# Feed-forward block of layer 1: the first two blocks of hidden channels are opened together, each with its two products that need half of the channels

## The chip, the cores and the metric

The kernel runs on one core of one Trainium2 chip, as a single program that computes the whole step. The metric is the device time of an execution in microseconds, as the median of the runs. The profile is one execution of the same program, taken by the hardware profiler on that core.

## The reference

One inference step of a decoder of two layers, for 512 prompt tokens and 8 sequences of 8 new tokens. Layer 0 mixes by a short convolution and attention to a memory, layer 1 by block-sparse attention with compressed, selected and sliding-window branches. Behind each mixer come an output projection, the residual, and a feed-forward block (FFN) of gated kind. What matters here is the part from the output projection to the end of a layer's FFN:

```python
D_MODEL = 1024
D_FF = 2816

def rmsnorm(x, g):
    y = x * lax.rsqrt(jnp.mean(x * x, axis=-1, keepdims=True) + RMS_EPS)
    return y * g

def swiglu(h, w_gu, w_dn):
    gate, up = jnp.split(h @ w_gu, 2, axis=-1)
    return (jax.nn.silu(gate) * up) @ w_dn

# in each layer, x is the residual of shape (tokens, 1024)
x = x + y @ w_o[l]
x = x + swiglu(rmsnorm(x, g_ffn[l]), w_gu[l], w_dn[l])
```

This is a cut in plain words of the functions, with the casts left out; all is float32.

## The kernel before, in words

**Layout.** The residual is held transposed: eight tiles `c.x[0]` to `c.x[7]` of 128 channels by 576 columns, a column for each of the 512 + 64 tokens. The columns are worked in two halves of 288. Every float32 product is made of three TensorE products: each operand is split into a high and a low part (`c.split`: ScalarE makes the high part at L185, VectorE the low part at L186), and high x high, high x low and low x high are summed in PSUM.

**The FFN's blocks.** `_ffn` goes through 22 blocks of the hidden channels (groups `FFG` of 4, 4, 4, 4, 3, 3). A block is 128 gate and 128 up channels, whose weights (1024 x 256) come in one load to `wq` (two buffers). `_seven` computes a block by seven products instead of eight: weights and columns are cut into two by two quarters, `a11` to `a22` for the weights (gate or up, lower or upper channels) and `b11` to `b22` for the columns (channels by half of the tokens), and each product takes a sum or difference of quarters on either side. A product is twelve matmuls of 128 x 128 by 128 x 288 (four slices of channels, three parts each) into one PSUM bank; the banks are taken by turns from the tags `d` and `s`, two banks each. The sums of weights are made by GpSimd in place (L723 to L728, `s3` having one buffer), each sum is split once more (L185, L186), and a product's result goes through `part` tiles (six of 288 columns): ScalarE copies it at L711, VectorE adds it at L715, GpSimd sums two at L735.

**The columns' side.** `_factors` makes seven factors `f[0]` to `f[6]` when they are first asked for: `b11`, `b21`, `t2`, `t3`, `t4`, `t1`, `b22`, with `t1 = b12 - b11` (tiles `ob` and `oa` hold their parts). The lower channels, `b11` and `b12`, come from the residual's tiles 0, 1, 4 and 5 only, so `f[0]` and `f[5]` need these four; all other factors need 2, 3, 6 and 7 as well. The output projection of layer 1, `_project_o`, goes through its columns in the order

```python
    for cc in (0, 2, 1, 3):
```

so that the tiles 0, 1, 4 and 5 are final before the last quarter of the projection runs.

**The root.** The norm's factor isn't multiplied into the columns but into the results: `evac` multiplies by the tile `rs` (L776 and L778, on GpSimd, with the sigmoid-weighted gate between them on ScalarE, L777), adds and multiplies on VectorE (L775, L780, L781), and splits the product for the second matrix. `rs` is made from the sums of squares by ten small matmuls (L230), a chain of small VectorE steps (L239 to L245, tile `rm`), five transposes on TensorE (L190) and copies on ScalarE and VectorE (L271, L274). In layer 0 it is made ahead of the FFN but for the copies; in layer 1 it is made when the first `evac` asks for it, in the middle of the first products.

**What sets the order.** Each engine runs its instructions in order. Which order that is, a scheduler of the tile framework decides when the program is built: it takes the code in the order in which it is written, and its own estimate of when operands and buffers come free, and lays down one list for each engine. More buffers, or code written in another order, can therefore move instructions that the diff doesn't name. The load of block j + 2's weights waits on SP's queue until the splits of block j have read `wq`. From the second group on, the second matrix's products of the group before (`dn`) are woven between a block's.

Of the kernel before, what the change touches and what calls it, by code (L numbers as in the profile page):

```python
# [22 lines left out]
KD = D // P  # L23
# [14 lines left out]
        "tmp": NT, "sq": NT, "rs": NT, "rm": 24, "sm": 32, "ss": 16, "sl": 16, "oa": NT, "ob": NT, "tf": 2 * NT,  # L38
        "wq": 2048, "wd": 1024, "bh": NT, "bl": NT, "wh": 512, "wl": 512, "s3": 512, "part": HALF, "ah": NT, "al": NT, "lh": 384, "ll": 384}
BUFS = {"x": 2, "v0": 4, "v1": 8, "v2": 8, "v3": 8, "raw": 2, "hi": 3, "lo": 3, "sp": 7, "pt": 4, "tmp": 3, "sq": 5,  # L40
        "rm": 2, "sm": 6, "ss": 6, "sl": 4, "oa": 14, "ob": 14, "tf": 7, "wq": 2, "wd": 2, "bh": 2, "bl": 2, "wh": 6, "wl": 6, "part": 6,
        "ah": 6, "al": 6, "lh": 8, "ll": 8}


# [636 lines left out]
    return pairs  # L681


def _seven(c, w, f, evac):


    nc = c.nc

    def quarter(a):
        a = a.rearrange("p (q h j) c -> p h q j c", h=2, j=2)  # L690
        return a[:, 0], a[:, 1]

    def unit(src):
        h, l = (c.t(t, dt=F32R).rearrange("p (q j c) -> p q j c", q=2, j=2) for t in ("wh", "wl"))
        c.split(h, l, src)
        return h, l

    def product(src, b):
        b = [b(q) for q in range(2)]
        u = unit(src)  # L700
        ps = c.psum(next(c.seven))[:, :HALF]
        for k in range(4):
            for x, y in ((0, 0), (0, 1), (1, 0)):
                nc.tensor.matmul(ps, u[x][:, k // 2, k % 2], b[k // 2][y][:, k % 2], start=(k == 0 and x + y == 0),  # L704
                                 stop=(k == 3 and x == 1))
        return ps

    def part(ps):
        t = c.t("part")
        nc.scalar.activation(t, ps, AF.Copy)  # L710
        return t  # L711

    def total(ps, t):
        out = c.t("part")
        nc.vector.tensor_tensor(out, ps, t, op=ALU.add)  # L715
        return out

    (a11, a12), (a21, a22) = quarter(w[:, :, :P]), quarter(w[:, :, P:])
    t1 = part(product(a11, f[0]))
    yield  # L720
    evac(0, 0, product(a12, f[1]), t1, c.t("part"))
    s3 = c.t("s3").rearrange("p (q j c) -> p q j c", q=2, j=2)
    nc.gpsimd.tensor_tensor(s3, a11, a21, op=ALU.subtract)  # L723
    nc.gpsimd.tensor_tensor(a21, a21, a22, op=ALU.add)
    nc.gpsimd.tensor_tensor(a11, a21, a11, op=ALU.subtract)  # L725
    yield
    u2 = total(product(a11, f[2]), t1)
    nc.gpsimd.tensor_tensor(a12, a12, a11, op=ALU.subtract)  # L728
    yield
    u3 = total(product(s3, f[3]), u2)  # L730
    yield
    evac(1, 0, product(a22, f[4]), u3, c.t("part"))
    yield
    t5 = part(product(a21, f[5]))
    nc.gpsimd.tensor_tensor(u2, u2, t5, op=ALU.add)  # L735
    yield
    evac(0, 1, product(a12, f[6]), u2, u2)
    evac(1, 1, u3, t5, t5)
    yield
# [16 lines left out]
def _ffn(c, layer, f, rs, op=()):  # L756
# [3 lines left out]
    w, wd = io["w_gu"][layer], io["w_dn"][layer]  # L760
    act = {}
    banks = itertools.cycle("tote")

    def gu(j):
        a = c.t("wq")
        nc.sync.dma_start(a, w[j])
        gt = c.t("tmp")
        tags = ("ah", "al") if j % 8 < 6 else ("bh", "bl")
        act[j] = h, l = [c.t(t, dt=F32R) for t in tags]

        def evac(m, n, x, y, out):
            o = slice(n * HALF, (n + 1) * HALF)
            g, r = gt[:, o], rs()[:, o]
            if m == 0:
                nc.vector.tensor_tensor(g, x, y, op=ALU.add)  # L775
                nc.gpsimd.tensor_tensor(g, g, r, op=ALU.mult)  # L776
# [2 lines left out]
            else:  # L779
                nc.vector.tensor_tensor(out, x, y, op=ALU.add)  # L780
                nc.vector.tensor_tensor(g, out, g, op=ALU.mult)  # L781
                c.split(h[:, o], l[:, o], g)
        return _seven(c, a.rearrange("p (k c) -> p k c", k=KD), f, evac)

    def acts(f0, f1):
        return [act[j][0] for j in range(f0, f1)], [act[j][1] for j in range(f0, f1)]
# [41 lines left out]

    left, pace, due = iter(()), 0.0, 0.0
    for i, (f0, f1) in enumerate(FFG):  # L830
        for j in range(f0, f1):
            for n, _ in enumerate(gu(j)):
                if i and j == f0 and n == 2:
                    left, pace, due = dn(*FFG[i - 1]), 16 / (7.0 * (f1 - f0) - 2), 0.0
                    next(left)
# [916 lines left out]
```

## Time and profile before

| what | us |
|---|---|
| median of 3 runs | 1660.23 (1657.28 to 1665.26) |
| the profiled execution, own time | 1662.34 |
| its span in the trace | 1660.6 |
| TensorE (PE) busy | 1590.8, 12036 matmuls |
| VectorE (DVE) busy | 1219.3 |
| ScalarE (ACT) busy | 783.5 |
| GpSimd (POOL) busy | 618.0 |

The mean granted clock of TensorE over the span is 0.982 of its full speed. Times in the trace count from the span's start. The first products of layer 0's FFN stand at about 372 us, those of layer 1's at about 1237 us. A busy time holds all the time that an instruction was in its engine, also what it spent there standing still.

### The profile page before, as it was taken

The numbers are of one execution on the slowest core, as the hardware profiler recorded it, in microseconds if no ns is written. First come the engines' busy times: TensorE is split into PE (matmuls) and PEld (weight loads), VectorE is DVE, ScalarE is ACT, GpSimd is POOL, SyncE is SP. The second block draws the span as 40 slices with busy tenths as digits, with TensorE's granted clock in tenths as the row PEclk, the third lists the DMA queues.
The fourth block names the chain that finished last, engine by engine and source line by source line (L and its number), as shares of the span: only waits on it lengthen the run. The fifth ranks groups of instructions, "written<-read, shape, count | busy, mean of one in ns | idle before, by whom it ended". The sixth has DMA issues, their size and how long they took to land.

```text
span 1660.6 us, 32051 instructions
## 1 busy us (share of the span) xinstructions
PE 1590.8 (96%) x12036; PEld 1477.6 (89%) x12036; DVE 1219.3 (73%) x2520; ACT 783.5 (47%) x1728; POOL 618.0 (37%) x652
## 2 busy tenths in 40 slices
PE   7999999998999999999999999999998999999996
PEld 7879999888999999998996866666898999999996
DVE  7665464749988888886456476787668988889886
ACT  5542242644344444443255376677645434444444
POOL 5011022318666565540000021121256756565541
PEclk8999999999999999999999999999998999999998
DMA  7412383242222322223145465665012132232221
GB/s 250 171 48 77 129 264 102 71 162 77 83 96 89 103 89 79 96 84 137 51 166 166 164 186 162 199 187 176 27 55 99 64 115 77 92 100 90 74 80 57
DMA packets 65348, 190.72 MB, mean 115 GB/s; under 512 B 9350, under 2 KB 16810, under 8 KB 54570
## 3 DMA queue, kind: packets, MB, share of 16 engines
q1 hardware_dynamic: 63848, 187.48, 34.0%
q8 instruction: 95, 1.56, 0.4%
q10 hardware_dynamic: 1346, 1.21, 0.3%
q14 instruction: 59, 0.48, 0.1%
HBM read 169.86 MB, written 18.80 MB: 114 GB/s over the span
## 4 chain that ended last, share of the span: by engine, by line
PE 84%; DVE 7%; DMA 3%; issue 2%; ACT 2%; SPq 0%; DVEq 0%; ACTq 0%
PE psd L704 14%; PE pss L704 14%; PE psd L197 6%; PE psd L198 6%; PE psd L199 6%; PE pss L461 4%; PE pso L1222 3%; PE pst L190 3%; PE pst L197 3%; PE pst L199 3%; PE pst L198 3%; PE psd L1165 2%; PE pse L1351 2%; PE pse L198 2%; PE pse L199 2%
## 5 line engine op out<-in xcount | busy, mean ns | idle before, releaser
L186 DVE TENSOR_TENSOR wl<-wq,wh 128x512 fp32r<-128x512 f32 x280 | 268.5, 966 | 19.2 <-ACT wh L185 13.3
L197 PE MATMUL psd<-v,hi 128*128 128x288 f32 (+2 forms) x720 | 216.4, 303 | 14.0 <-ACT hi L185 7.8
L198 PE MATMUL psd<-v,hi 128*128 128x288 f32 (+2 forms) x720 | 215.9, 300 | 2.6 <-DVE v L295 2.5
L199 PE MATMUL psd<-v,lo 128*128 128x288 f32 (+2 forms) x720 | 215.3, 300 | 2.1 <-DVE lo L186 2.1
L185 ACT ACTIVATE wh<-wq 128x512 fp32r<-128x512 f32 x280 | 169.6, 623 | 88.3 <-PE psd L704 25.9
L197 PEld LDWEIGHTS psd<-v,hi 128*128 128x128 f32 (+1 forms) x720 | 136.7, 191 | 18.9 <-ACT hi L185 7.9
L198 PEld LDWEIGHTS psd<-v,hi 128*128 128x128 f32 (+1 forms) x720 | 137.3, 191 | 5.7 <-DVE v L295 3.3
L199 PEld LDWEIGHTS psd<-v,lo 128*128 128x128 f32 (+1 forms) x720 | 136.9, 191 | 5.1 <-DVE lo L186 2.7
L704 PE MATMUL psd<-ob,wh 128*128 128x288 f32 x616 | 127.7, 298 | 5.1 <-DVE tmp L775 3.3
L704 PE MATMUL psd<-oa,wh 128*128 128x288 f32 x616 | 127.6, 298 | 2.7 <-DVE part L715 2.4
L704 PE MATMUL pss<-oa,wh 128*128 128x288 f32 x616 | 128.1, 299 | 2.0 <-DVE part L715 2.0
L704 PE MATMUL pss<-ob,wh 128*128 128x288 f32 x616 | 127.0, 297 | 2.8 <-DVE part L715 0.9
L781 DVE TENSOR_TENSOR tmp<-part,tmp 128x288 f32<-128x288 f32 x88 | 89.4, 1015 | 53.6 <-POOL tmp L778 49.4
L776 POOL TENSOR_TENSOR tmp<-tmp,rs 128x288 f32<-128x288 f32 x88 | 95.5, 1085 | 84.6 <-DVE tmp L775 84.5
L185 ACT ACTIVATE hi<-raw 128x1024 fp32r<-128x1024 f32 (+3 forms) x60 | 59.9, 1003 | 119.3 <-PE psd L198 104.3
L704 PEld LDWEIGHTS psd<-ob,wh 128*128 128x128 f32 x616 | 100.1, 190 | 6.5 <-DVE tmp L775 3.7
L704 PEld LDWEIGHTS psd<-oa,wh 128*128 128x128 f32 x616 | 100.4, 191 | 3.9 <-issue 1.9
L704 PEld LDWEIGHTS pss<-ob,wh 128*128 128x128 f32 x616 | 99.8, 190 | 4.3 <-DVE ob L186 1.2
L704 PEld LDWEIGHTS pss<-oa,wh 128*128 128x128 f32 x616 | 101.3, 192 | 2.4 <-DVE part L715 2.4
L186 DVE TENSOR_TENSOR lo<-raw,hi 128x1024 fp32r<-128x1024 f32 (+3 forms) x60 | 75.3, 1261 | 26.0 <-ACT hi L185 25.8
L777 ACT ACTIVATE part<-tmp 128x288 f32<-128x288 f32 x88 | 39.2, 445 | 114.0 <-POOL tmp L776 113.8
L725 POOL TENSOR_TENSOR wq<-wq 128x512 f32<-128x512 f32 x44 | 59.2, 1346 | 89.5 <-DVE wl L186 89.5
(474 smaller groups left out, 4950.8 us busy)
## 6 DMA issues: line engine op xcount, KB each, us to landing
wq<-in_w_gu SPq DMA_DIRECT2D x44, 1024.0 KB
g<-in_cmp_pages SPq DMA_DIRECT2D x64, 256.0 KB
wd<-in_w_dn SPq DMA_DIRECT2D x32, 512.0 KB
raw<-in_w_in_a SPq DMA_DIRECT2D x9, 1024.0 KB
v<-in_cache_mem_kv SPq DMA_DIRECT2D x32, 256.0 KB
x<-in_slc_pages SPq DMA_DIRECT2D x32, 256.0 KB
raw<-in_slc_pages SPq DMA_DIRECT2D x32, 256.0 KB
wd<-in_w_dn SPq DMA_DIRECT2D x16, 384.0 KB
```

Of the source, the lines that this page charges most:

```text
L185: self.nc.scalar.activation(hi, src, AF.Copy)
L186: (eng or self.nc.vector).tensor_tensor(lo, src, hi.bitcast(F32), op=ALU.subtract)
L190: self.nc.tensor.transpose(out, in_, self.ident[:k, :k])
L197: nc.tensor.matmul(out, wh, xh, start=(k == 0), stop=False)
L198: nc.tensor.matmul(out, wh, xl, start=False, stop=False)
L199: nc.tensor.matmul(out, wl, xh, start=False, stop=(k == n - 1))
L461: nc.tensor.matmul(ps[:, :n], w[kv][i][:, lt, 2 * kp + k], x[j][:, k, lt:lt + n], start=(kp + k + lt + i + j == 0), stop=(kp == 3 and k + ...
L704: nc.tensor.matmul(ps, u[x][:, k // 2, k % 2], b[k // 2][y][:, k % 2], start=(k == 0 and x + y == 0), stop=(k == 3 and x == 1))
L725: nc.gpsimd.tensor_tensor(a11, a21, a11, op=ALU.subtract)
L776: nc.gpsimd.tensor_tensor(g, g, r, op=ALU.mult)
L781: nc.vector.tensor_tensor(g, out, g, op=ALU.mult)
L1222: nc.tensor.matmul(po()[64 * s:64 * s + 64, :P], v, w, start=(i + j == 0), stop=(i == 1 and j == len(todo) - 1))
```

## The change

For the first two blocks of layer 1, `_ffn` starts both at once, and by turns: first product of block 0, of block 1, then a second one of block 0 and of block 1. With `early`, `_seven` takes as its second product `t5 = a21' x f[5]` (`a21'` being the sum of L724) and `a12 x f[1]` behind it, with the first `evac`; without it `t5` stays where it was, the sixth. All 22 blocks of both layers go through the same code, but `early` is set for these two alone. `part` has eight buffers instead of six, `s3` two instead of one, in both layers, and the gate's tile `gt` is taken when the first `evac` needs it, after `rs`. No instruction is added or taken away, and none changes in size.

```diff
--- before.py
+++ after.py
@@ -38,7 +38,7 @@
-        "rm": 2, "sm": 6, "ss": 6, "sl": 4, "oa": 14, "ob": 14, "tf": 7, "wq": 2, "wd": 2, "bh": 2, "bl": 2, "wh": 6, "wl": 6, "part": 6,
+        "rm": 2, "sm": 6, "ss": 6, "sl": 4, "oa": 14, "ob": 14, "tf": 7, "wq": 2, "wd": 2, "bh": 2, "bl": 2, "wh": 6, "wl": 6, "part": 8, "s3": 2,
@@ -681,7 +681,8 @@
-def _seven(c, w, f, evac):
+def _seven(c, w, f, evac, early=False):
@@ -718,10 +719,15 @@
     (a11, a12), (a21, a22) = quarter(w[:, :, :P]), quarter(w[:, :, P:])
     t1 = part(product(a11, f[0]))
     yield
-    evac(0, 0, product(a12, f[1]), t1, c.t("part"))
+    if not early:
+        evac(0, 0, product(a12, f[1]), t1, c.t("part"))
     s3 = c.t("s3").rearrange("p (q j c) -> p q j c", q=2, j=2)
     nc.gpsimd.tensor_tensor(s3, a11, a21, op=ALU.subtract)
     nc.gpsimd.tensor_tensor(a21, a21, a22, op=ALU.add)
+    if early:
+        t5 = part(product(a21, f[5]))
+        yield
+        evac(0, 0, product(a12, f[1]), t1, c.t("part"))
     nc.gpsimd.tensor_tensor(a11, a21, a11, op=ALU.subtract)
     yield
     u2 = total(product(a11, f[2]), t1)
@@ -730,8 +736,10 @@
     u3 = total(product(s3, f[3]), u2)
     yield
     evac(1, 0, product(a22, f[4]), u3, c.t("part"))
-    yield
-    t5 = part(product(a21, f[5]))
+    if not early:
+        yield
+    if not early:
+        t5 = part(product(a21, f[5]))
     nc.gpsimd.tensor_tensor(u2, u2, t5, op=ALU.add)
     yield
     evac(0, 1, product(a12, f[6]), u2, u2)
@@ -761,16 +769,17 @@
     act = {}
     banks = itertools.cycle("tote")
 
-    def gu(j):
+    def gu(j, early=False):
         a = c.t("wq")
         nc.sync.dma_start(a, w[j])
-        gt = c.t("tmp")
+        gt = _Lazy(lambda: c.t("tmp"))
         tags = ("ah", "al") if j % 8 < 6 else ("bh", "bl")
         act[j] = h, l = [c.t(t, dt=F32R) for t in tags]
 
         def evac(m, n, x, y, out):
             o = slice(n * HALF, (n + 1) * HALF)
-            g, r = gt[:, o], rs()[:, o]
+            r = rs()[:, o]
+            g = gt()[:, o]
             if m == 0:
...
@@ -780,7 +789,7 @@
...
-        return _seven(c, a.rearrange("p (k c) -> p k c", k=KD), f, evac)
+        return _seven(c, a.rearrange("p (k c) -> p k c", k=KD), f, evac, early)
@@ -828,8 +837,14 @@
 
     left, pace, due = iter(()), 0.0, 0.0
     for i, (f0, f1) in enumerate(FFG):
+        ahead = []
+        if layer == 1 and i == 0:
+            ahead = [gu(j, True) for j in range(2)]
+            for _ in range(2):
+                for g in ahead:
+                    next(g)
         for j in range(f0, f1):
-            for n, _ in enumerate(gu(j)):
+            for n, _ in enumerate(ahead.pop(0) if ahead else gu(j)):
                 if i and j == f0 and n == 2:
                     left, pace, due = dn(*FFG[i - 1]), 16 / (7.0 * (f1 - f0) - 2), 0.0
                     next(left)
```

The lists of the engines show what this moves at three places. A name carries its tile's number, which the two kernels count differently. Lines up to L684 have the same number in both; behind it the changed kernel's are 1 to 9 higher (L704 is L705, L723 is L725, L776 is L785).

On GpSimd, at the opening of layer 0's FFN (`wq_475` holds block 0's weights there, `wq_507` block 1's), the list was:

```order
L723 TENSOR_TENSOR s3_487_4737<-wq_475_4691 128x512
L724 TENSOR_TENSOR wq_475_4691<-wq_475_4691 128x2x2x128
L725 TENSOR_TENSOR wq_475_4691<-wq_475_4691 128x2x2x128
L728 TENSOR_TENSOR wq_475_4691<-wq_475_4691 128x2x2x128
L723 TENSOR_TENSOR s3_519_4893<-wq_507_4847 128x512
L776 TENSOR_TENSOR tmp_476_4693<-tmp_476_4693,rs_472_4637 128x288
L724 TENSOR_TENSOR wq_507_4847<-wq_507_4847 128x2x2x128
L778 TENSOR_TENSOR tmp_476_4693<-part_486_4732,rs_472_4637 128x288
L725 TENSOR_TENSOR wq_507_4847<-wq_507_4847 128x2x2x128
```

And it is now:

```order
L725 TENSOR_TENSOR s3_487_4737<-wq_475_4691 128x512
L725 TENSOR_TENSOR s3_519_4893<-wq_507_4847 128x512
L726 TENSOR_TENSOR wq_475_4691<-wq_475_4691 128x2x2x128
L726 TENSOR_TENSOR wq_507_4847<-wq_507_4847 128x2x2x128
L731 TENSOR_TENSOR wq_475_4691<-wq_475_4691 128x2x2x128
L734 TENSOR_TENSOR wq_475_4691<-wq_475_4691 128x2x2x128
L785 TENSOR_TENSOR tmp_486_4732<-tmp_486_4732,rs_472_4637 128x288
L731 TENSOR_TENSOR wq_507_4847<-wq_507_4847 128x2x2x128
L787 TENSOR_TENSOR tmp_486_4732<-part_485_4731,rs_472_4637 128x288
```

The two sums of block 1 (L723 and L724, now L725 and L726) stand ahead of the third sum of block 0 and of its first multiplication by `rs_472`, where the first of them stood behind four of block 0 and the second behind that multiplication.

On TensorE, at the opening of layer 1's FFN, the first row of each product is given, from the first product behind the projection to the transposes (`oa` and `ob` are the factors' parts). It was:

```order
L704 MATMUL psd_2460_15970<-ob_2453_15955,wh_2458_15966 128x288
...
L704 MATMUL pss_2470_16003<-ob_2463_15988,wh_2468_15999 128x288
...
L704 MATMUL psd_2486_16079<-ob_2480_16061,wh_2484_16075 128x288
...
L230 MATMUL pss_2472_16017<-ones_2_68,tmp_2395_15499 128x1
...
L704 MATMUL pss_2495_16110<-ob_2489_16097,wh_2493_16106 128x288
L704 MATMUL psd_2504_16140<-oa_2498_16127,wh_2502_16136 128x288
...
L704 MATMUL pss_2512_16170<-oa_2506_16158,wh_2510_16166 128x288
...
L190 MATMUL pst_2475_16036<-ident_1_63,rm_2473_16028 128x128 x4
...
L704 MATMUL psd_2520_16198<-oa_2514_16186,wh_2518_16194 128x288
```

And it is now:

```order
L705 MATMUL psd_2462_15973<-ob_2455_15958,wh_2460_15969 128x288
...
L705 MATMUL pss_2466_15992<-ob_2455_15958,wh_2464_15988 128x288
...
L705 MATMUL psd_2476_16029<-oa_2470_16014,wh_2474_16025 128x288
...
L705 MATMUL pss_2481_16051<-oa_2470_16014,wh_2479_16047 128x288
...
L705 MATMUL psd_2491_16084<-ob_2484_16069,wh_2489_16080 128x288
...
L230 MATMUL pss_2493_16098<-ones_2_68,tmp_2395_15499 128x1
...
L705 MATMUL psd_2515_16182<-ob_2509_16169,wh_2513_16178 128x288
L705 MATMUL pss_2506_16151<-ob_2500_16136,wh_2504_16147 128x288
...
L705 MATMUL psd_2532_16243<-oa_2526_16231,wh_2530_16239 128x288
L705 MATMUL pss_2524_16212<-oa_2518_16199,wh_2522_16208 128x288
...
L190 MATMUL pst_2496_16117<-ident_1_63,rm_2494_16109 128x128 x4
...
L705 MATMUL pss_2535_16278<-ob_2484_16069,wh_2533_16274 128x288
```

There were 72 matmuls of `_seven` ahead of the first transpose (row 7792 of TensorE's list) and there are 103 (row 7823); the ten small matmuls of L230 stood inside the third product, from behind 27 matmuls on, and stand behind the fifth product's twelfth, behind 60.

On VectorE, at the same opening, around the first step of the root's chain (L239); `wq_2448` is block 0 of layer 1. Rows 1909 to 1918 were:

```order
L186 TENSOR_TENSOR wl_2519_16195<-wq_2448_15947,wh_2518_16194 128x512
L775 TENSOR_TENSOR tmp_2449_15949<-pss_2470_16003,part_2461_15983 128x288
L649 TENSOR_TENSOR tf_2497_16125<-v0_2465_15992,tf_2478_16053 128x576
L186 TENSOR_TENSOR wl_2526_16235<-wq_2521_16229,wh_2525_16234 128x512
L186 TENSOR_TENSOR ob_2483_16072<-tf_2478_16053,ob_2482_16071 128x576
L186 TENSOR_TENSOR oa_2492_16103<-tf_2488_16095,oa_2491_16102 128x576
L186 TENSOR_TENSOR ob_2490_16098<-tf_2488_16095,ob_2489_16097 128x576
L239 TENSOR_SCALAR rm_2473_16028<-pss_2472_16017 128x5
L186 TENSOR_TENSOR oa_2499_16128<-tf_2497_16125,oa_2498_16127 128x576
L186 TENSOR_TENSOR oa_2501_16133<-tf_2497_16125,oa_2500_16132 128x576
```

And rows 1914 to 1925 are now:

```order
L186 TENSOR_TENSOR ob_2503_16144<-tf_2499_16132,ob_2502_16143 128x576
L186 TENSOR_TENSOR oa_2512_16175<-tf_2508_16167,oa_2511_16174 128x576
L186 TENSOR_TENSOR wl_2531_16240<-wq_2448_15947,wh_2530_16239 128x512
L186 TENSOR_TENSOR ob_2510_16170<-tf_2508_16167,ob_2509_16169 128x576
L784 TENSOR_TENSOR tmp_2498_16126<-psd_2491_16084,part_2463_15986 128x288
L186 TENSOR_TENSOR oa_2519_16200<-tf_2517_16197,oa_2518_16199 128x576
L186 TENSOR_TENSOR wl_2534_16275<-wq_2451_15951,wh_2533_16274 128x512
L186 TENSOR_TENSOR wl_2539_16299<-wq_2451_15951,wh_2538_16298 128x512
L186 TENSOR_TENSOR oa_2521_16205<-tf_2517_16197,oa_2520_16204 128x576
L239 TENSOR_SCALAR rm_2494_16109<-pss_2493_16098 128x5
L186 TENSOR_TENSOR oa_2527_16232<-v0_2483_16066,oa_2526_16231 128x576
L186 TENSOR_TENSOR oa_2529_16236<-v0_2486_16073,oa_2528_16235 128x576
```

L239 was row 1916 and is row 1923, the last split of block 0's weights was row 1909 (`wl_2519`) and is row 1916 (`wl_2531`), and the last step of the chain, L245, is row 1930 in both.

## Rows read from the trace of the kernel before

**Rows 1.** The page's part 1: busy time and share of the span, by engine

```profile
PE 1590.8 (96%) x12036; PEld 1477.6 (89%) x12036; DVE 1219.3 (73%) x2520; ACT 783.5 (47%) x1728; POOL 618.0 (37%) x652
```

**Rows 2.** Table by stage: stretch, length, busy us by engine (instructions), granted clock, DMA share, GB/s

```profile
372.33:425.00 52.67, 45.51 (x309) 43.97 (x308) 50.66 (x63) 23.46 (x47) 42.88 (x33) 0.94 0.23 82
1237.50:1258.90 21.40, 16.37 (x99) 14.74 (x97) 20.51 (x32) 13.26 (x24) 8.55 (x7) 0.84 0.29 99
1243.70:1248.00 4.30, 3.11 (x9) 1.96 (x9) 4.30 (x6) 4.13 (x8) 1.67 (x1) 0.66 0.70 246
1258.90:1277.84 18.94, 18.90 (x131) 18.93 (x132) 13.47 (x22) 9.76 (x20) 12.79 (x12) 0.91 0.17 56
1277.84:1292.03 14.19, 12.54 (x87) 11.44 (x85) 13.90 (x18) 6.02 (x13) 11.47 (x10) 1.00 0.21 74
1300.31:1600.00 299.69, 299.69 (x2251) 299.45 (x2252) 259.51 (x400) 127.11 (x258) 176.69 (x153) 1.00 0.27 88
```

**Rows 3.** TensorE in time, layer 1's opening: start, length, instruction, [idle before <- releaser]

```profile
1244.99 0.57 PE L704 MATMUL pss<-ob,wh 128*128 128x288 f32 x1 [0.75 <-ACT ob L185]
...
1257.41 0.76 PE L190 MATMUL pst<-ident,rm 128*128 128x128 f32 x5 [2.65 <-DVE rm L245]
1258.94 0.82 PE L704 MATMUL psd<-oa,wh 128*128 128x288 f32 x2 [0.77 <-DVE part L715]
```

**Rows 4.** The chain of waits behind the transposes: start, us, what

```profile
1258.94 3.22 PE psd L704 x12
...
1263.80 1.60 PE psd L704 x12
```

**Rows 5.** VectorE in time, layer 1's opening

```profile
1223.56 0.76 DVE L186 TENSOR_TENSOR ob<-v,ob 128x576 fp32r<-128x576 f32 x1 [1.32 <-ACT ob L185]
...
1248.33 0.15 DVE L239 TENSOR_SCALAR rm<-pss 128x5 f32<-128x5 f32 x1
...
1256.13 1.22 DVE L245 SCALAR_TENSOR_TENSOR rm<-rm 128x5 f32<-128x5 f32 x1
...
1261.36 1.04 DVE L781 TENSOR_TENSOR tmp<-part,tmp 128x288 f32<-128x288 f32 x1 [1.58 <-POOL tmp L778]
...
1263.65 0.68 DVE L186 TENSOR_TENSOR wl<-wq,wh 128x512 fp32r<-128x512 f32 x1
...
1289.26 2.85 DVE L186 TENSOR_TENSOR wl<-wq,wh 128x512 fp32r<-128x512 f32 x2
```

**Rows 6.** GpSimd in time, the same stretch

```profile
1255.61 1.72 POOL L723 TENSOR_TENSOR s<-wq 128x512 f32<-128x512 f32 x1 [1.97 <-DVE rm L244]
...
1260.53 0.80 POOL L778 TENSOR_TENSOR tmp<-part,rs 128x288 f32<-128x288 f32 x1 [0.96 <-ACT part L777]
...
1288.91 1.45 POOL L723 TENSOR_TENSOR s<-wq 128x512 f32<-128x512 f32 x1 [2.16 <-DVE wl L186]
1290.31 1.25 POOL L735 TENSOR_TENSOR part<-part,part 128x288 f32<-128x288 f32 x1
```

**Rows 7.** GpSimd in time, layer 0's opening

```profile
365.03 1.29 POOL L724 TENSOR_TENSOR wq<-wq 128x512 f32<-128x512 f32 x1
367.67 1.29 POOL L725 TENSOR_TENSOR wq<-wq 128x512 f32<-128x512 f32 x1 [1.36 <-DVE wl L186]
...
373.83 1.68 POOL L723 TENSOR_TENSOR s<-wq 128x512 f32<-128x512 f32 x1 [2.87 <-DVE wl L186]
...
376.69 1.74 POOL L724 TENSOR_TENSOR wq<-wq 128x512 f32<-128x512 f32 x1
```

**Rows 8.** VectorE in time, layer 0's opening

```profile
366.84 0.69 DVE L186 TENSOR_TENSOR wl<-wq,wh 128x512 fp32r<-128x512 f32 x1 [4.65 <-PE pss L461]
...
372.33 0.68 DVE L186 TENSOR_TENSOR wl<-wq,wh 128x512 fp32r<-128x512 f32 x1
...
373.67 6.52 DVE L186 TENSOR_TENSOR wl<-wq,wh 128x512 fp32r<-128x512 f32 x5
```

**Rows 9.** SP's queue in time: the load of block 2's weights

```profile
1243.70 0.33 SPq L766 DMA_DIRECT2D wq<-in_w_gu  x1
```

## Prediction

> **What bounds the kernel now.** The page's busy times come first: TensorE works 1590.8 of 1660.6 us [rows 1], so some 70 us of its time are free, and the question is whether the change touches any of them. The table by stage [rows 2] answers where. In the opening of layer 0's FFN (372.33 to 425.00) TensorE is busy 45.51 of 52.67 us, so 7.2 us are lost. In that of layer 1 it is busy 16.37 of 21.40 us at a granted clock of 0.84 (1237.50 to 1258.90), then without a gap at 0.91 to 1277.84, then 12.54 of 14.19 us in one block's period (1277.84 to 1292.03), and much the same to 1300.31. From 1300.31 to 1600.00 it is busy 299.69 of 299.69 us. So what is gained before 1300.31 should still be there at the end: behind it nothing of TensorE's is idle that could swallow it.
>
> TensorE's instructions in order of time say what it waits for in layer 1's opening [rows 3]: an activation's high half (ScalarE, 0.75 us), the last step of the inverse root (L245 on VectorE, 2.65 us), a PSUM bank that L715 on VectorE frees (0.77 us). The chain of waits [rows 4] gives the two prices of a product of twelve matmuls: 3.22 us just after the long wait, at the low clock, and 1.60 us at full clock.
>
> All of these waits end at VectorE or at what it feeds, so VectorE's own pace is next [rows 5], beside GpSimd's [rows 6]. A split of 512 columns takes 0.68 us when GpSimd is quiet (1263.65), and two in a row start 0.60 us apart then, so 1.28 us. The two at 1289.26 took 2.85 us, while GpSimd ran L723 and L735; and L735, 1.25 us there, is of the size of L778, which took 0.80 us. So each stands still for the other. Their busy times in one block's period are 13.90 and 11.47 us of 14.19 [rows 2]; both contain waiting. I laid the two engines' rows over each other (without VectorE's that read PSUM, which do not slow): from 1219 to 1300 at least one of the two is running, but for ten moments of 4.8 us together. The first is the 0.99 us that end at 1223.56, the largest behind the restart the 0.96 us before 1260.53 [rows 5, 6]. **This pair, not TensorE, sets the pace of the openings.**
>
> The Trainium skill ("SBUF — State Buffer", section "SBUF: two separate sides") states it as a rule: the two engines share a port pair under an exclusive lock, taken for a whole instruction by a GpSimd operation or by a VectorE operation with two SBUF inputs, and the loser blocks. By it the two splits at 1289.26 would take the 1.10 us that L723 still had, plus 0.80 for L735, plus 1.36, so 3.26 us where the row has 2.85: nearly the whole lock. The rule speaks against this change, which alters the order of such work and not its amount: by it layer 1's opening can give back 4.8 us at most, where without it the 7.6 us of the first rival would be open.
>
> **The change part by part.** It adds no instruction and takes none away; the buffers (`part` 8, `s3` 2) and the late `gt` cost nothing by themselves, but they free the scheduler, in layer 0 too.
>
> *Layer 0.* Only the buffers act there. On GpSimd, L723 and L724 of block 1 move ahead of most of block 0's work (first pair of order rows). Before, they ran at 373.83 and 376.69 for 1.68 and 1.74 us [rows 7], in the middle of VectorE's five splits, which took 6.52 us [rows 8] where five alone take 4 x 0.60 + 0.68 = 3.08 us. Their new place is in GpSimd's gaps of 1.36 and 2.87 us [rows 7]. Both engines stood together 0.52 us at 366.32 (between the end of L724 and VectorE's split at 366.84) and 1.15 us up to 372.33: 1.67 us to fill. The bounds are 0 (on ScalarE the copy of `rs`, L271, now stands behind two more splits of weights, and L776 waits for it) and the two instructions' own time, 2 x 1.29 = 2.6 us. I take the idle that the rows show: **-1.7 us**.
>
> *Layer 1, products.* Ahead of the transposes of the root (L190) TensorE now has 103 matmuls of `_seven` instead of 72 (second pair of order rows): 31 matmuls, 31/12 x 1.60 = 4.1 us of work that the wait for the root no longer holds up. But they are of use only if the following products are fed, and these need the same splits as before. Ahead of the root's copy on VectorE stand 14 splits of weights instead of 12, and on GpSimd one more of block 1's sums (the a11 sum) is done before the last projection ends: 2 x 0.60 + 1.29 = 2.5 us of the pair's work moved forward, into the waits before 1237.5. Behind the root the same 14 GpSimd instructions, from the first multiplication by `rs` of block 0 to the first of block 2, run in either order. The bounds are 0 (the moved work only displaces other work) and the 4.8 us of common idle. I take **-2.4 us**, half of that, which is also what the moved work amounts to.
>
> *The root's sums.* The ten small matmuls (L230) are now behind 60 products' matmuls instead of in the middle of the third product, and VectorE's first step on their result, L239, stands 7 rows later (third pair of order rows). At 20.51/32 = 0.64 us a row [rows 2] that is 4.5 us: 1252.8 instead of 1248.33 [rows 5]. L245 keeps its place, 1930th row in both. I cost it at nothing as long as L239 comes before 1252.6 (the third rival says why).
>
> *The loads.* SP's queue has the same order. Block 2's load must wait for block 0's last split, also 7 rows later on VectorE (row 1916 for 1909): 1243.70 [rows 9] becomes 1248.2. The whole of it was through in the stretch of 4.30 us behind its issue (246 GB/s x 4.30 us = 1.06 MB) [rows 2], so the data are there by 1252.5, and GpSimd first needs them near 1255.61 [rows 6]: hidden, with 3 us to spare. Without that cover each us late is one more us at the head of GpSimd's queue.
>
> **Sum.** The profiled execution took 1662.34 us: 1662.34 - 1.7 - 2.4 = 1658.2. It lies 2.1 us above the median of the three runs, 1660.23; against the median the forecast is **1656 us**, 0.25% faster. About 0.5%, 8.3 us, is what a measurement of this kernel can tell from no change.
>
> **Rivals.**
> 1. *TensorE's lead counts in full.* For it: TensorE is without a gap from 1258.90 to 1277.84, so a lead at the restart is not eaten at once, and VectorE idles 1.58 us before 1261.36 [rows 5]. Then layer 1 returns the 5.0 us lost before 1258.90 and the 1.65 us a period of 14.19 us from 1277.84 to 1300.31, 2.6 us: 7.6 us, and layer 0 its 1.7: 1660.2 - 9.3 = 1651. Against it: the common idle of the pair.
> 2. *The change doesn't do what it says.* The two blocks' follow-up work, put off behind the root, runs up against the same lock, and block 1's next product waits for a bank that L715 of block 0 frees, as before. Nothing moves: 1660.
> 3. *Slower: the root comes late.* TensorE must now do the twelve matmuls of block 0's a22 and six more before the transposes, and the twelve need the bank that L239 frees. At the low clock 18 matmuls are 18 x 3.22/12 = 4.8 us, so with L239 after 1257.41 - 4.8 = 1252.6 the root is late, and with it all that is multiplied by `rs`. L239 can be as late as 1257.35 - 3 x 0.68 = 1255.3 (three splits stand between it and L245's end): 2.7 us late, 1663, with none of the gains.
>
> **How the numbers follow.** The forecast has 0.52 (it needs the lock, which the rows show well, and order rows that I have counted), the first rival 0.18, the second 0.17, the third 0.13. The likeliest case's own range is 1653 to 1659, from its bounds (-7.4 and 0) narrowed by half. To leave out no more than two in ten I take in most of the first rival and the third up to 1663: **1650 to 1663**. Faster by over 0.5% (below 1651.9) is most of the first rival and the far end of the forecast, 0.16; slower by over 0.5% (above 1668.5) needs more than the third rival's price, 0.05; the rest, 0.79, is within 0.5%.
>
> **What would show it.** In the changed profile: GpSimd's L725 and L726 of block 1 of layer 0 done before 372, and the five splits behind them in about 4 us; four products back to back behind the last projection of layer 1; the transposes there within 0.5 us of where they are now, counted from the projection's end; and TensorE's last wait of the opening ended some 4 us sooner counted from the kernel's start, then no gap to 1600. The prediction is wrong if GpSimd and VectorE still leave idle moments of 4 us or more in that stretch while TensorE waits (then the order is worse than I think), if TensorE's gaps past 1277 vanish (first rival), or if the transposes come 2 us later (third).

## The result, and the profile after

The changed kernel takes 1674.48 us (median of 6 runs, 1672.46 to 1678.78) beside 1661.45 us of the kernel before (median of 6): 1.0080 times as long, 95% interval 1.0065 to 1.0096. It is 13 us slower, where 1656 us and a range of 1650 to 1663 had been forecast. Ratios, here and below, leave out executions that were slowed as a whole (one of early_own_p6 took 2978 us). The page's head, its busy times, and the shares of its chain of waits:

```profile
span 1674.1 us, 32002 instructions
...
PE 1593.5 (95%) x12036; PEld 1475.8 (88%) x12036; DVE 1162.4 (69%) x2520; ACT 773.0 (46%) x1728; POOL 607.6 (36%) x652
...
PE 54%; DVE 16%; POOL 11%; DMA 7%; issue 7%; ACT 4%; SPq 1%; DVEq 0%; ACTq 0%; POOLq 0%
```

The shares of the chain before were:

```profile
PE 84%; DVE 7%; DMA 3%; issue 2%; ACT 2%; SPq 0%; DVEq 0%; ACTq 0%
```

Against [rows 1] TensorE has the same 12036 matmuls and 2.7 us more of busy time, in a span that is 13.5 us longer. VectorE's busy time *fell* by 57 us with the same 2520 instructions. In the chain of waits TensorE has 54% where it had 84%, DMA 7% where it had 3%, and GpSimd 11%, which wasn't in it before. Where the time went is in the table by stage (columns as in [rows 2], stretches laid from the same first product):

```profile
372.57:425.24 52.67, 46.71 (x332) 45.34 (x331) 50.69 (x66) 23.68 (x48) 41.02 (x32) 0.97 0.25 82
425.00:600.00 175.00, 170.48 (x1271) 168.33 (x1271) 131.47 (x222) 70.20 (x148) 97.80 (x88) 1.00 0.26 85
1244.10:1265.50 21.40, 19.19 (x135) 18.62 (x133) 21.30 (x31) 14.41 (x28) 9.00 (x5) 0.92 0.27 99
1265.50:1284.44 18.94, 17.21 (x111) 17.11 (x111) 17.20 (x23) 9.35 (x18) 15.89 (x14) 0.82 0.17 56
1284.44:1298.63 14.19, 11.80 (x78) 11.56 (x77) 14.19 (x19) 5.65 (x13) 10.44 (x10) 0.88 0.23 74
1306.91:1606.60 299.69, 293.59 (x2185) 290.91 (x2184) 216.61 (x382) 118.81 (x250) 165.47 (x148) 1.00 0.27 87
```

From 425 to 600 the kernel before has:

```profile
425.00:600.00 175.00, 175.00 (x1325) 175.00 (x1324) 150.53 (x235) 73.74 (x153) 107.38 (x93) 1.00 0.28 91
```

The openings are hardly better: layer 0's holds 46.71 us of TensorE's work instead of 45.51, layer 1's first stretch 19.19 instead of 16.37, but layer 1's three stretches together hold 324 matmuls instead of 317. And the last row had 299.69 busy us of 299.69 before [rows 2] and has 293.59; from 425 to 600 there are 4.5 idle us of 175 and 54 matmuls fewer, where the kernel before has no gap. **The running part, which the prediction took as closed, has holes.** The table of GpSimd's waits, in layer 0's FFN (360 to 760) and then in layer 1's (1230 to 1640), says what stands at the bottom of most of it (us in total, times, longest):

```profile
POOL tmp L785 <- DVE tmp L784: 52.7, 39, 2.7
POOL s L725 <- DMA wq<-in_w_gu: 51.5, 16, 5.8
...
POOL s L725 <- DMA wq<-in_w_gu: 49.2, 16, 5.5
```

In each layer GpSimd waits 16 times, some 50 us in all, for a load of weights. The kernel before has no such wait in either stretch. Of layer 0's eight gaps of TensorE behind 425 (6.14 us in all), six stand 4 to 7 us behind the end of such a wait (4.56 us); the other ten waits leave no gap, and the first two gaps come ahead of all of them (more on these below). One of the waits, followed through four queues in order of time (SP's, GpSimd's, VectorE's, TensorE's):

```profile
562.89 0.33 SPq L774 DMA_DIRECT2D wq<-in_w_gu  x1
...
564.24 1.30 POOL L731 TENSOR_TENSOR wq<-wq 128x512 f32<-128x512 f32 x1 [1.96 <-DVE wl L186]
567.88 1.29 POOL L725 TENSOR_TENSOR s<-wq 128x512 f32<-128x512 f32 x1 [2.34 <-DMA wq<-in_w_gu]
569.13 1.75 POOL L734 TENSOR_TENSOR wq<-wq 128x512 f32<-128x512 f32 x1
570.84 1.28 POOL L726 TENSOR_TENSOR wq<-wq 128x512 f32<-128x512 f32 x1
572.08 0.80 POOL L743 TENSOR_TENSOR part<-part,part 128x288 f32<-128x288 f32 x1
...
572.91 0.46 DVE L789 TENSOR_TENSOR part<-part,part 128x288 f32<-128x288 f32 x1 [2.82 <-POOL part L743]
573.28 0.45 DVE L784 TENSOR_TENSOR tmp<-pss,part 128x288 f32<-128x288 f32 x1
...
573.88 0.50 PE L705 MATMUL pss<-ob,wh 128*128 128x288 f32 x2 [1.24 <-DVE tmp L784]
```

Read it from the top. The load is issued at 562.89. At 565.54 GpSimd comes to L725, the `s3` sum of the *next* block, and stands still 2.34 us until the load has landed. Behind it in GpSimd's list are this block's own sums, L734 and L743. L743 ends at 572.9; VectorE, in its own order, waits 2.82 us for it with L789, and behind L789 stands L784, which frees a PSUM bank; TensorE waits 1.24 us for that bank. An estimate from these rows: without the 2.34 us L743 would have ended at 570.5, VectorE would have waited 0.5 us for it, and TensorE not at all. GpSimd's list shows why the sum came so early. For the same block of layer 0 it was before (L728 and L735 are L734 and L743 now):

```
L725 TENSOR_TENSOR wq_807_6411<-wq_807_6411 128x2x2x128
L728 TENSOR_TENSOR wq_807_6411<-wq_807_6411 128x2x2x128
L735 TENSOR_TENSOR part_783_6270<-part_783_6270,part_799_6351 128x288
L776 TENSOR_TENSOR tmp_768_6205<-tmp_768_6205,rs_472_4637 128x288
L723 TENSOR_TENSOR s3_864_6699<-wq_848_6633 128x512
```

and it is now:

```
L731 TENSOR_TENSOR wq_807_6411<-wq_807_6411 128x2x2x128
L725 TENSOR_TENSOR s3_864_6699<-wq_848_6633 128x512
L734 TENSOR_TENSOR wq_807_6411<-wq_807_6411 128x2x2x128
L726 TENSOR_TENSOR wq_848_6633<-wq_848_6633 128x2x2x128
L743 TENSOR_TENSOR part_783_6270<-part_783_6270,part_799_6351 128x288
```

The sum into `s3_864`, which needs the load into `wq_848`, stood behind block `wq_807`'s last two sums and stands ahead of them. With one `s3` buffer it could not: the buffer was still held by block 807's own `s3`, until its split had been made. The second buffer removed that hold, and the scheduler used it.

### The profile page after: what moved, and what is told of

The parts are those of the page before. It is cut to its first block, busy times and chain, and to the rows that moved or that the text cites. A ratio compares the mean times of both kernels' runs of the same rounds, so it can differ in the third digit from the quotient of the medians.

```text
span 1674.1 us, 32002 instructions
## 1 busy us (share of the span) xinstructions
PE 1593.5 (95%) x12036; PEld 1475.8 (88%) x12036; DVE 1162.4 (69%) x2520; ACT 773.0 (46%) x1728; POOL 607.6 (36%) x652
## 4 chain that ended last, share of the span: by engine, by line
PE 54%; DVE 16%; POOL 11%; DMA 7%; issue 7%; ACT 4%; SPq 1%; DVEq 0%; ACTq 0%; POOLq 0%
PE psd L197 6%; PE psd L198 6%; PE psd L199 6%; DVE wl L186 5%; PE pss L461 4%; PE pss L705 4%; PE psd L705 4%; DMA wq<-in_w_gu 4%; PE pso L1237 3%; PE pst L190 3%; PE psd L1180 2%; POOL s L725 2%; POOL tmp L785 2%; POOL wq L734 2%; POOL wq L726 2%
## 5 line engine op out<-in xcount | busy, mean ns | idle before, releaser
L186 DVE TENSOR_TENSOR wl<-wq,wh 128x512 fp32r<-128x512 f32 x280 | 246.4, 887 | 56.8 <-ACT wh L185 50.4
L705 PE MATMUL pss<-ob,wh 128*128 128x288 f32 x616 | 129.3, 301 | 13.0 <-DVE tmp L784 9.9
L785 POOL TENSOR_TENSOR tmp<-tmp,rs 128x288 f32<-128x288 f32 x88 | 97.6, 1110 | 107.2 <-DVE tmp L784 102.3
L705 PE MATMUL psd<-ob,wh 128*128 128x288 f32 x616 | 128.2, 299 | 7.1 <-DVE tmp L784 5.6
L705 PE MATMUL psd<-oa,wh 128*128 128x288 f32 x616 | 127.5, 298 | 2.8 <-DVE part L716 2.4
L705 PE MATMUL pss<-oa,wh 128*128 128x288 f32 x616 | 125.6, 295 | 0.0
L705 PEld LDWEIGHTS pss<-ob,wh 128*128 128x128 f32 x616 | 100.9, 192 | 15.8 <-issue 7.0
L725 POOL TENSOR_TENSOR s<-wq 128x512 f32<-128x512 f32 x44 | 63.8, 1450 | 140.3 <-DMA wq<-in_w_gu 103.0
L705 PEld LDWEIGHTS psd<-ob,wh 128*128 128x128 f32 x616 | 100.4, 191 | 9.3 <-issue 4.6
L705 PEld LDWEIGHTS psd<-oa,wh 128*128 128x128 f32 x616 | 100.6, 191 | 3.3 <-DVE part L716 2.6
L705 PEld LDWEIGHTS pss<-oa,wh 128*128 128x128 f32 x616 | 99.5, 189 | 0.0
L705 PE MATMUL pss<-ob,wl 128*128 128x288 f32 x308 | 93.4, 303 | 0.0
```

The source lines that it names most:

```text
L186: (eng or self.nc.vector).tensor_tensor(lo, src, hi.bitcast(F32), op=ALU.subtract)
```

## The experiments

The length of an FFN in a trace, from the start of its first product to the end of its last matmul of a product (layer 0: 367.62 to 745.22 before, 367.86 to 752.91 after; layer 1: 1237.51 to 1622.11 and 1244.11 to 1635.43), is a sharper measure than the whole time: the two traces of the kernel before agree to 0.03 us (how far that goes is said at the end of this section). Each ratio is against executions of the kernel before from the same measurement, whose median was 1660.62 to 1661.96 us. All runs:

| kernel | median us | ratio to before, 95% interval | FFN 0, us | FFN 1, us | GpSimd's waits for a load, layer 0 / 1, us |
|---|---|---|---|---|---|
| before (trace shown above) | 1661.45 | | 377.60 | 384.60 | 0 / 0 |
| before_again (one run) | 1657.90 | | 377.57 | 384.59 | 0 / 0 |
| after | 1674.48 | 1.0080 (1.0065 to 1.0096) | 385.05 | 391.32 | 51.5 / 49.2 |
| s3_only | 1676.71 | 1.0094 (1.0078 to 1.0109) | 388.13 | 393.21 | 51.6 / 55.7 |
| bufs_only | 1677.35 | 1.0088 (1.0054 to 1.0123) | 386.78 | 392.52 | 53.0 / 51.9 |
| s33_wq3 | 1678.33 | 1.0106 (1.0090 to 1.0121) | 387.20 | 392.28 | 42.7 / 51.2 |
| part_only | 1655.11 | 0.9962 (0.9948 to 0.9975) | 375.63 | 384.04 | 0 / 0 |
| part_again | 1656.94 | 0.9976 (0.9960 to 0.9992) | 375.63 | 384.07 | 0 / 0 |
| early_own_s3 | 1656.05 | 0.9971 (0.9959 to 0.9984) | 375.66 | 384.01 | 0 / 0.3 |
| early_own_p6 | 1660.05 | 0.9986 (0.9974 to 0.9998) | 377.07 | 382.98 | 0 / 0.2 |
| mixed | 1655.94 | 0.9963 (0.9949 to 0.9977) | 375.63 | 383.08 | 0 / 0.2 |
| s3_wq3 | 1660.76 | 0.9999 (0.9985 to 1.0012) | 379.22 | 385.77 | 0 / 0 |
| after_wq3 | 1657.65 | 0.9986 (0.9972 to 1.0000) | 376.63 | 384.00 | 0 / 0 |
| after_pinned | 1709.21 | 1.0284 (1.0250 to 1.0318) | 404.23 | 401.75 | 0 / 4.6 |
| after_pin_r | 1660.90 | 1.0002 (0.9990 to 1.0013) | 378.86 | 384.35 | 0 / 0 |

**Which part of the change costs.** Each buffer alone, on the kernel before:

```diff
-"part": 6,
+"part": 6, "s3": 2,
```

and

```diff
-"part": 6,
+"part": 8,
```

> The kernel before with one edit: s3 has two buffers. Theory A (the second buffer lets the scheduler put the next block's s3 sum ahead of this block's last two sums in GpSimd's list, where it waits for the next block's load): all of the loss is here, 1672 to 1678 us against 1661, with 15 to 16 waits of GpSimd for the load of wq in each layer, 45 to 55 us of them in each, and each layer's FFN 6 to 8 us longer. Theory B (the loss comes from the two blocks opened together: their phase, or the late tile gt): 1659 to 1663, no such waits. Theory C (the eight part buffers): 1659 to 1663 too.

> The kernel before with one edit: part has eight buffers instead of six. Theory A and theory B: same as before, 1659 to 1663, no wait of GpSimd for a load. Theory C (more part buffers let work run in a worse order): 1670 or more.

The second `s3` buffer alone makes 15 us; the FFNs are 10.5 and 8.6 us longer, more than the 6 to 8 that were expected. Eight `part` buffers alone make the kernel *faster*, which no theory had said. Theory A stands on this, B and C fall. Both buffers without the early opening (bufs_only, `"part": 8, "s3": 2`):

> The buffers of the change alone (part eight, s3 two), with no block opened early. Theory A: the whole loss without the opening's part of it, 1673 to 1677, layer 0's FFN 385.0 us as in the changed kernel, layer 1's 1 to 2 us longer than there (391.3).

It is as slow as s3_only, and its second FFN is 1.2 us longer than the changed kernel's, the side on which the early opening should show. Its first is 1.8 us longer than expected, although the lists of layer 0 are those of the changed kernel, row for row. The trace shows where: behind a gap of 1.61 us TensorE's granted clock is 0.50 (1.2 of 2.4 GHz) from 648.3 to 651.7, with 15 matmuls in those 3.4 us, where the changed kernel runs 24 at 1.00 at the same place. From there on it is 1.7 us behind. s3_only has the same stretch, so some 1.7 of its 10.5 us should be of this kind.

**The change without the second buffer.** The opening needs two `s3` tiles at once. `s3` goes back to one buffer, and the second block gets a tile `s4` that nobody else uses (only the lines that choose the tile are shown):

```diff
-    s3 = c.t("s3").rearrange("p (q j c) -> p q j c", q=2, j=2)
+    s3 = c.t(own).rearrange("p (q j c) -> p q j c", q=2, j=2)
...
-        return _seven(c, a.rearrange("p (k c) -> p k c", k=KD), f, evac, early)
+        return _seven(c, a.rearrange("p (k c) -> p k c", k=KD), f, evac, early, "s4" if early and j == 1 else "s3")
```

> The changed kernel with s3 back at one buffer; the second of the two blocks opened together has its s3 sum in a tile of its own, which no other block uses. All else is as in the changed kernel: both blocks opened together, eight part buffers, the late gt. Theory A: GpSimd's list has its old order from the third block on, no wait for loads there, and only the gain of layer 1's opening is left, some 2 us (what the changed kernel led by at its 200th to 400th product matmul of layer 1): 1658 to 1661. Theory B: 1672 or more, as the changed kernel.

It came out at 1656.05, below the expected 1658 to 1661. The loss is gone with the opening still there, so the opening isn't its cause. But its FFNs are those of part_only to 0.03 us, 384.01 beside 384.04 in layer 1: with eight `part` buffers the early opening gives nothing. The opening by itself has the same edit with `"part": 6`:

> The two blocks opened together, the second with its own s3 tile (s3 one buffer elsewhere), but six part buffers as before: the early opening by itself. If the opening is limited by VectorE and GpSimd and gives nothing by itself: as before, 1659 to 1663, layer 1's FFN 384.0 to 384.6 us long. If the gain of 2.4 us that was forecast is there: 1657 to 1660, with that FFN below 382.5 us.

Layer 1's FFN takes 382.98 us, 1.6 us less than before, between the two expectations. So the opening is worth 1.6 us with six `part` buffers and nothing with eight; the two together give less in layer 1 than the opening alone.

Could TensorE's clock be what ate the opening's lead? In the changed kernel it was lower in layer 1's second and third stretch (0.82 and 0.88, before 0.91 and 1.00). A later run, mixed (below), has the lists of early_own_p6 in layer 1, row for row. Over the first 68.3 us of that FFN both traces hold 414 matmuls, early_own_p6 at a granted clock of 0.98, mixed at 0.90, and the FFNs take 382.98 and 383.08 us. So no: in this opening TensorE isn't what sets the pace.

**The sum's place, or the wait in that place?** First try: three buffers each for `s3` and `wq`.

> The kernel before with three buffers each for s3 and wq. GpSimd's list has the same order inside a block as with two s3 buffers (the next block's s3 sum ahead of this block's last two sums), but the load of a block's weights can start one block earlier. Theory A, in the form that the wait for the load is what costs: the sum waits for no load, and the time is that of before or up to 4 us less, 1657 to 1663. Rival A2 (the order costs by itself: the last two sums come later by the s3 sum's own 1.3 us and VectorE's order changes with them): as slow as with two s3 buffers, 1670 or more.

The time was A2's, but the run doesn't test A2: with three buffers the scheduler puts the sum *two* blocks ahead (the sum for `wq_889` between the last two sums of `wq_807`), so that it again waits for its load, 42.7 and 51.2 us. My expectation had read the pattern of the list without the block numbers. Two buffers for `s3` and three for `wq` put the sum two blocks ahead too, but behind the last sums of the block that runs, and so some sums later:

> The kernel before with two buffers for s3 and three for wq. GpSimd's list puts the s3 sum of a block still further ahead, before all sums of the block in front of it, but the load that it needs starts a block earlier too. Theory A (only the wait for the load costs, not the sum's place): GpSimd waits for no load in the running part of either layer (0 instead of some 50 us a layer), TensorE has no gap there, and the time is 1655 to 1663. Rival A2 (a sum that runs ahead of the previous block's own sums costs by its place, whatever it waits for): 1670 or more, with VectorE's waits for L735 at 20 us or more from 425 to 700.

TensorE has no gap in the running part of either layer (and the table of GpSimd's waits has no load):

```profile
425.00:600.00 175.00, 175.00 (x1322) 174.79 (x1321) 151.00 (x235) 73.77 (x154) 107.37 (x93) 1.00 0.28 91
1310.00:1600.00 290.00, 290.00 (x2182) 290.00 (x2182) 248.54 (x388) 124.13 (x251) 167.43 (x144) 1.00 0.27 87
```

The sum for `wq_889` now runs ahead of the last two sums of `wq_848`, the block in front of it, and costs nothing there, since its load is in. So A2 falls as the account of the whole loss. It isn't out everywhere: no run has the changed kernel's own order, with the sum ahead of the *running* block's last sums, and all loads in. At one place in each layer the changed kernel itself has it, ahead of the running part's first wait for a load: L725 and L726 of the next block stand ahead of L743, their load is in, and TensorE has gaps of 0.47 and 1.11 us in layer 0 (at 426.6 and 428.9) and of 0.45 and 1.08 us in layer 1 (at 1308.1 and 1310.4). These some 1.5 of the 6 idle us a layer may be the order's own. The 2.8 us that s3_wq3's two FFNs are longer than before lie in the openings (layer 0 is 0.3 us behind after 100 matmuls, 1.4 after 200 and 1.6 from the 400th on). The changed kernel itself with `"wq": 3`:

> The changed kernel with three buffers for wq and nothing else changed. Theory A: the wait for the load is gone, and what is left is what eight part buffers give: 1654 to 1659. Rival A2, or theory B (the early opening's phase costs later): 1668 or more.

1657.65: the wait and the loss are gone.

**The changed kernel with only the order mended.** Here the buffers and loads stay as they are, and a false dependence holds the next sum back (not shown: the next block then takes `c.next_s3` as its `s3` tile). First behind the block's last sum of products:

```diff
     nc.gpsimd.tensor_tensor(u2, u2, t5, op=ALU.add)
+    if not last:
+        c.next_s3 = c.t("s3")
+        nc.gpsimd.tensor_copy(c.next_s3[:, 0:1], u2[:, 0:1])
```

> The changed kernel with both s3 buffers and two wq buffers, where the next block's s3 tile is taken right behind this block's last GpSimd sum (u2 + t5) and one column of that sum is copied into it (one small GpSimd instruction a block is added). So the next block's s3 sum can't be put ahead of this block's sums. Theory A: no wait for a load in GpSimd's list, and with the small copies (some 0.1 us each, off TensorE's path) 1654 to 1661. If the s3 sum's place were not the cause: 1672 or more.

It took 1709 us, a miss; the copies took 0.44 us each on average instead of 0.1. The scheduler now lays `u2 + t5` itself at the end of the block, and everything of the next block behind it (layer 0):

```profile
POOL part L743 <- ACT part L711: 111.9, 18, 8.1
```

The head of GpSimd's list waits for ScalarE's copy of TensorE's product instead of a load, and more than twice as long. So this run doesn't test the sum's place; it has put another wait at the head of the list. Then behind the last sum of *weights*, which waits for no product:

```diff
     nc.gpsimd.tensor_tensor(a12, a12, a11, op=ALU.subtract)
+    if not last:
+        c.next_s3 = c.t("s3")
+        nc.gpsimd.tensor_copy(c.next_s3[:, 0:1], a12[:, 1, 1, 127:128])
```

> The changed kernel with both s3 buffers and two wq buffers, where the next block's s3 tile is taken right behind this block's last sum of weights (the one that lays a11 off a12) and one column of it is copied into the tile (one GpSimd instruction of some 0.5 us a block is added). So the s3 sum stands behind this block's sums of weights in every block, and behind its sum of products in most. Theory A: GpSimd's waits for the load fall from 50 us a layer to under 15, and with them the loss: 1655 to 1663. Rival (the second s3 buffer costs in another way than by the sum's place ahead of this block's sums): 1670 or more.

1660.90 us, and neither layer has a wait for a load of `wq`. TensorE's stretches:

```profile
425.00:600.00 175.00, 173.15 (x1305) 172.69 (x1306) 145.04 (x234) 77.23 (x153) 111.73 (x102) 1.00 0.27 91
1310.00:1600.00 290.00, 290.00 (x2182) 290.00 (x2181) 237.07 (x387) 125.34 (x247) 177.78 (x162) 1.00 0.28 90
```

With the same two `s3` and two `wq` buffers, one dependence a block takes 13.6 us back. The fair measure of what it gives back is early_own_s3, which differs from the changed kernel in the second `s3` buffer: the buffer adds 16.7 us to the two FFNs, and the dependence takes 13.2 of them back. So the second buffer costs, for the most part, by the order that it allows and not by being there. Of the 3.5 us that stay, 3.2 are in layer 0, with gaps of 0.75 and 1.10 us at 426.7 and 429.3, where two sums of the next block still stand ahead of this block's sum of products; what makes the rest stays open.

**How much is scatter, and the best version.**

> The kernel before once more, for the scatter of one trace against another. If the 2 us that eight part buffers took off layer 0's FFN are theirs, its FFN is again 377.3 to 377.9 us long here (375.6 in both runs with eight part buffers); what differs ahead of it, 364.9 to 367.9 us over the runs so far, is scatter.

> Eight part buffers alone, once more: its first measurement was 6.4 us below before, while its two FFNs are 2.5 us shorter in the trace. If the FFNs are all of it: 1658 to 1660 against 1660.6 of before. If the larger gain is real: 1653 to 1656.

> The best of each layer in one kernel: eight part buffers in layer 0, six in layer 1, the two blocks opened together with the second's s3 tile its own. From the traces: layer 0's FFN 375.6 us, layer 1's 383.0 us, together 3.6 us less than before: 1657 against 1660.6 of before. If the two don't add up (layer 1's FFN at 384.0 as with eight part buffers): 1658 to 1660.

The FFNs often repeat to 0.03 us (377.57 for 377.60; 375.63 to 375.66 in four traces with eight `part` buffers in layer 0), but not always: early_own_p6, whose lists of layer 0 are those of the kernel before, took 377.07. The kernel before has a granted clock of 0.50 from 419.0 to 422.4, with 16 matmuls in 3.3 us where early_own_p6 has 27. So 1.4 to 2.0 us in layer 0 are the `part` buffers' own. What lies ahead of the first FFN starts it at 364.86 (before_again) or 367.62 in the same program. Eight `part` buffers took 6.4 us off the median in one measurement and 5.0 in the other, their FFNs 2.5 in these traces; whether the rest is scatter between measurements stays open (the second interval reaches down to 1.3 us). mixed (eight `part` buffers in layer 0, six and the opening in layer 1) has the shortest FFNs, as expected, but its median, 1655.94, can't be told from part_only's. The simplest version that beats both kernels is the one number: `"part": 8`.

## Why the prediction was wrong

**The step that failed** is the sentence that the buffers "cost nothing by themselves, but they free the scheduler, in layer 0 too", which was then costed in the two openings alone. It rested on [rows 2], "behind it nothing of TensorE's is idle that could swallow it". That is true of the kernel before, and says nothing of the changed one, whose lists differ in all of the running part. The move stood in the lists already: among the 14 GpSimd instructions behind layer 1's root, which the prediction counted as the same in either order, the next block's sum into `s3_2597` was tenth and is fifth, ahead of the running block's last sum of weights. Counted over all of TensorE's matmuls from an FFN's first product on, the changed kernel is 0.4 us ahead at the 800th in layer 0 and 0.5 in layer 1; then it falls behind gap by gap, and from the 2000th on it is 7.45 and 6.72 us behind. The FFNs together are 7.45 + 6.72 = 14.2 us longer, the median 13.0. The term put at nothing was the second `s3` buffer's: alone it costs 15 us (s3_only), by a sum that waits for its load ahead of work that the other engines need.

**The mechanism had been named, at one place.** "Without that cover each us late is one more us at the head of GpSimd's queue" was said of block 2's load in layer 1's opening, and there it nearly held: the load was issued 4.6 us later counted from the first product (forecast: 4.5), and GpSimd waited 0.30 us for it, where 3 us had been thought to be spare. It should have been asked of the other loads: what stands ahead of the `s3` sum in GpSimd's list, in a block of the middle? In the kernel before the sum of a block comes 9.4 us behind the load's issue (557.68 and 567.11 at one block); after, GpSimd is there 2.6 us behind it.

**Layer 0's opening, -1.7.** GpSimd's sums of block 1 did run before 372 (the prediction's list of signs says layer 1 there; 372 lies in layer 0), and five splits of VectorE stand within 3.7 us:

```profile
363.62 2.53 POOL L725 TENSOR_TENSOR s<-wq 128x512 f32<-128x512 f32 x2 [31.55 <-DMA smtab<-in_tab]
366.11 2.98 POOL L726 TENSOR_TENSOR wq<-wq 128x512 f32<-128x512 f32 x2
...
374.37 0.68 DVE L186 TENSOR_TENSOR wl<-wq,wh 128x512 fp32r<-128x512 f32 x1
...
375.11 2.98 DVE L186 TENSOR_TENSOR wl<-wq,wh 128x512 fp32r<-128x512 f32 x4
```

TensorE was 2.9 us ahead at its 200th matmul and 0.4 at its 400th. The move alone, which the second `s3` buffer allows, gives nothing that lasts: s3_only makes it too, and is 1.1 us ahead at the 200th and 1.5 behind at the 400th. Eight `part` buffers alone keep 1.4 to 2.0 us, with the `s3` sum of block 1 still behind four instructions of block 0. So a gain of the forecast size exists, but it isn't the one that was argued for: that the number fits is luck.

**Layer 1's products, -2.4.** The transposes came 20.07 us behind the first product instead of 19.90, and L239 3.4 us later than before (forecast: 4.5), so the root wasn't late and the third rival is out. (By its own numbers the prediction should have given it more: 1252.8 forecast for L239 is behind the 1252.6 up to which it cost nothing.) The four products ran back to back, and the lead was there and was eaten:

```profile
1264.18 0.76 PE L190 MATMUL pst<-ident,rm 128*128 128x128 f32 x5 [1.65 <-DVE rm L245]
1267.34 0.85 PE L705 MATMUL pss<-ob,wh 128*128 128x288 f32 x2 [1.73 <-DVE part L716]
...
1289.93 0.85 PE L705 MATMUL psd<-oa,wh 128*128 128x288 f32 x2 [2.39 <-DVE part L716]
```

The last two gaps are waits for banks that VectorE frees late (such a gap stands in [rows 3] with 0.77 us). At the 200th matmul 2.0 us of lead were left, at the 400th 0.5. Alone the opening is worth 1.6 us (early_own_p6) and beside eight `part` buffers nothing: the term was the right kind, a third too large at best, and its lower bound was the true value with those buffers. The first rival, the lead in full, is out in every run.

**VectorE and GpSimd.** That this pair, not TensorE, sets the pace of layer 1's opening agrees with mixed and early_own_p6, which differ there in TensorE's clock alone. But it didn't set the running part: over the whole span VectorE's busy time went *down* 57 us (from 425 to 600 from 150.53 to 131.47) while TensorE waited more. By the Trainium skill ("SBUF — State Buffer", section "SBUF: two separate sides") the loser blocks while the other has the shared ports. If a busy time holds this standing, as the splits of [rows 5] suggest, the fall agrees with that; no run here separates it from other reasons.

## What to carry to other kernels

A second buffer is not only room: it is an order that the scheduler wasn't allowed before. When a pool grows, compare every engine's list in a block of the *running* part, not just where the edit is meant to act, and look for an instruction that now waits for a load ahead of work that others need; on an engine that runs in order everything behind it pays. A kernel whose bound engine shows no gap has cover for small losses only as long as the lists stay as they are.

If a bigger pool makes a kernel slower, first look what the head of each queue waits for, then hold the moved instruction back with a dependence that is ready early: the same trick on a result that comes late left the kernel 47 us slower than the one before.

## What the runs showed that was not expected

Eight `part` buffers instead of six, a lesser part of the change, are worth 0.24 to 0.38% by themselves (2.5 us of the FFNs in the traces), more than the opening that they were to serve (1.6 us). A GpSimd copy of one column, 128x1, took 0.44 us on average in after_pinned and 0.37 in after_pin_r (spans of single ones from 0.17 to 0.66), against 1.29 us for a sum of 512 columns that is not held up. And 3.4 us at half of TensorE's clock cost 1.7 us in the running part (bufs_only beside the changed kernel), while in layer 1's opening, where it waits for others anyhow, 10 us more at half the clock cost 0.1 us (mixed beside early_own_p6). And VectorE's busy time for the same work differs by 57 us between two orders, so a fall in busy time is no sign of a faster kernel.
